# A two-layer hybrid network on one core: the down phase gives VectorE the accumulation alone, and products use six PSUM banks

## The chip, the cores and the metric

The kernel runs on one core of a Trainium2 chip. Five engines work in parallel, each through its own queue in order: TensorE (PE; its weight loads are shown as PEld), VectorE (DVE), ScalarE (ACT), GpSimd (POOL), and SyncE (SP), which here issues nearly all transfers. The metric is the device time of one execution in microseconds (us), the median over runs. "Granted clock" is the share of its full clock that TensorE was given in a stretch.

## The reference

A sequence of 16 learned tokens and 1024 inputs of width 1024 goes through two layers. Each adds a mixer (stick-breaking attention beside an S5 state space model in layer 0, a gated delta rule in layer 1) and then an MLP, all with RMS norms around them. The change concerns the MLP:

```python
def sq_relu_mlp(h, w1, w2):
    return jnp.square(jax.nn.relu(h @ w1)) @ w2

for i in range(DEPTH):
    ...
    hn = rms_norm(hs, pre_mlp_norm[i])
    hs = hs + rms_norm(sq_relu_mlp(hn, mlp_w1[i], mlp_w2[i]), post_mlp_norm[i])
```

`w1` is 1024 x 4096 and `w2` 4096 x 1024, in fp32.

## The kernel before

Activations lie with features on the 128 partitions and tokens along the row: 1040 tokens in layer 0, the last 1024 in layer 1. A matrix product keeps fp32 accuracy by splitting each operand into a high part (the value cast to fp32r) and a low part (the value minus its high part) and adding three matmuls: high x high (L176), high weights x low activations (L177), low weights x high activations (L178). Making one operand takes a cast and a subtraction.

The MLP of a layer (`mlp`, L401) has three phases:

- *Up*: six of the 32 blocks of 128 hidden features go through `up` (L416). A product sums over eight input blocks in one PSUM bank, and VectorE takes relu and scale out of the bank (L422, into a tile `t1`, shown as `t`). Meanwhile `halves_T` makes sums and differences of the inputs (`th`, `tl`) for the next phase.
- *Pairs*: the other 26 blocks are made two at a time by `pair` with seven half-size products instead of eight (L476 to L478). ScalarE casts the weight operands (L437), GpSimd subtracts (L438), VectorE combines the products (L485, L489). These products go round the banks of all three kinds. The squared result goes to `hd` in DRAM.
- *Down*: `down` (L531) is called 14 times with two hidden blocks each and once more with the last four (`last`). Each call loads its hidden blocks (`hidden`, L523: DMA of `hr`, ScalarE's cast to `hh`, VectorE's subtraction to `hl`) and its weights (`weight`, L152: DMA of `wraw`, VectorE's cast to `whi`, GpSimd's subtraction to `wlo`), and then runs over eight blocks of output features. A product is six matmuls (two hidden blocks, three each) in one bank: three products of 352, 344 and 344 tokens per output block in layer 0, two of 512 in layer 1. Call 0 copies each product to `acc` on ScalarE (L550); the later ones add it to `acc` on VectorE (L552).

PSUM has eight banks: three named `mm`, three `tr`, two `ax`. `gemm` (L182), which both up and down use, takes `mm` alone, so a product can start when the product three before it has been taken out. There are two tiles `wraw` and four each of `whi` and `wlo`, so a call's weights are made while the call before it runs; 33 slots hold `hr`, `hh`, `hl` and `acc` with others, so hidden blocks run several calls ahead.

A scheduling layer sets the order on each engine: it spreads the instructions by its own estimate of when each will be ready, and adds the waits. Line numbers below are those of this kernel; a line that many callers share (L165, L166, L176 to L178, L228, L229) stands for all of them, so tile names tell them apart.

Of the kernel before, what the change touches and what calls it, by code (L numbers as in the profile page):

```python
# [19 lines left out]
NT = 1040  # L20
# [26 lines left out]
def f(ap):  # L47
    return ap.bitcast(F32)


class Net:
# [97 lines left out]
    def raw(self):  # L149
        return self.sb.tile([128, NT], F32, tag="wraw", name="wraw", bufs=2)  # L150

    def weight(self, src, n=1024, spare=False, fast=False):  # L152

        nc = self.nc
        raw = self.raw()
        nc.sync.dma_start(raw[:, :n], src)
        if spare:
            hi, lo = self.slot("whi", F32R), self.slot("wlo", F32R)
        else:
            hi = self.sb.tile([128, 1024], F32R, tag="whi", name="whi", bufs=4)  # L160
            lo = self.sb.tile([128, 1024], F32R, tag="wlo", name="wlo", bufs=4)
        if fast and HA:
            nc.scalar.copy(hi[:, :n], raw[:, :n])
        else:
            nc.vector.tensor_copy(hi[:, :n], raw[:, :n])  # L165
        (nc.vector if fast else nc.gpsimd).tensor_sub(lo[:, :n], raw[:, :n], f(hi[:, :n]))  # L166
        return hi, lo
# [11 lines left out]
            self.clock += n / 800  # L179
            self.beat()  # L180

    def gemm(self, mts, kts, wap, rhs, chunks, order, evac, hook=None):  # L182
        mts = list(mts)
        cs = range(len(chunks))
        todo = [(m, c) for m in mts for c in cs] if order == "m" else [(m, c) for c in cs for m in mts]
        for i, (m, c) in enumerate(todo):
            if order == "c" and i == len(mts) * (len(chunks) - 1) and hook is None:
                self.finish()
            o, n = chunks[c]
            pt = self.mm()  # L190
            self.unit(pt[:, :n], kts, lambda k: wap(m, k), rhs, o, n)
            evac(m, c, pt[:, :n])
            if hook is not None:
                hook(m, c)
# [206 lines left out]
    def mlp(self, layer, st, hs_d, chunks, gpre, ahead=None):  # L401

        nc = self.nc
        w1, w2 = self.io["w1"], self.io["w2"]
        hd = self.dr.tile([128, 32, NT], F32, tag="hd%d" % layer, name="hd", bufs=1)
        hid = {}
        t0, h = (0, 520) if layer == 0 else (16, 512)
        half = ((0, 260), (260, 260)) if layer == 0 else ((0, 512),)
        wide = chunks if layer == 0 else CH4

        def put(m, o, n, x):

            nc.scalar.activation(x[:, :n], x[:, :n], AF.Square)
            nc.sync.dma_start(hd[:, m, o:o + n], x[:, :n])

        def up(ms, order):  # L416
            W = self.w_up if ms[0] == 0 else {m: self.weight(w1[layer, m]) for m in ms}

            def ev(m, c, pt):
                o, n = chunks[c]  # L420
                t1 = self.tmp("t1")
                nc.vector.scalar_tensor_tensor(t1[:, :n], pt, 0.0, st["rb"][:, o:o + n], op0=ALU.max, op1=ALU.mult)  # L422
                put(m, o, n, t1)

            self.gemm(ms, range(8), lambda m, k: tuple(w[:, k * 128:(k + 1) * 128] for w in W[m]), lambda k: (st["hi"][k], st["lo"][k]), chunks, order, ev)

        room = []
        bank = cycle((self.mm, self.tr, self.mm, self.tr, self.mm, self.tr, self.ax))
# [32 lines left out]
        def pair(ma, mb, T):  # L461
# [26 lines left out]
            def block(m, o, n, x):  # L488
                nc.vector.scalar_tensor_tensor(x[:, :n], x[:, :n], 0.0, st["rb"][:, o:o + n], op0=ALU.max, op1=ALU.mult)  # L489
                put(m, o, n, x)  # L490
# [32 lines left out]
        def hidden(k):  # L523

            raw = self.slot("hr")
            hi, lo = self.slot("hh", F32R), self.slot("hl", F32R)
            nc.sync.dma_start(raw[:, t0:NT], hd[:, k, t0:NT])
            self.split(hi[:, t0:NT], lo[:, t0:NT], raw[:, t0:NT])
            hid[k] = (hi, lo)

        def down(ks, last=False):  # L531
            first = ks[0] == 0
            for k in ks:
                hidden(k)
            W = {k: self.weight(w2[layer, k]) for k in ks}
            out, hook, ch = None, None, wide
            if last:
                ch = chunks
                if ahead is None:
                    ch = CH3  # L540
                if ahead is not None:
                    ahead()
                ssq = self.slot("ssq_o")
                reuse = [t for k in ks for t in hid[k]]
                *out, hook = self.residual(acc, ssq, reuse, G_POSTMLP + 8 * layer, hs_d, gpre, ch)

            def ev(m, c, pt):
                o, n = ch[c]
                if first:
                    nc.scalar.copy(acc[m][:, o:o + n], pt)  # L550
                else:
                    nc.vector.tensor_add(acc[m][:, o:o + n], pt, acc[m][:, o:o + n])  # L552
                if last:
                    self.sq_acc(ssq, m, m == 0, acc[m][:, o:o + n], o, n)

            self.gemm(range(8), ks, lambda m, k: tuple(w[:, m * 128:(m + 1) * 128] for w in W[k]), lambda k: hid[k], ch, "c" if last else "m", ev, hook)
            for k in ks:
                del hid[k]
            return out

        up([0, 1, 2, 3], "c")
        T = self.halves_T(st, hs_d, t0, h, G_PREMLP + 8 * layer)
        for m in range(4, UPC):
            up([m], "m")
        for m in range(UPC, 32, 2):
            pair(m, m + 1, T)
        acc = [self.slot("acc") for _ in range(8)]
        for g in range(14):
            down([2 * g, 2 * g + 1])
        return down([28, 29, 30, 31], True)  # L570


# [317 lines left out]
    def glu(self):  # L890

        nc = self.nc
        W = [self.weight(self.io["wglu"][i]) for i in range(2)]
        hact = self.hact
# [14 lines left out]

        wap = lambda m, k: tuple(w[:, 512 * (k % 2) + 128 * m:512 * (k % 2) + 128 * m + 128] for w in W[k // 2])  # L910
        for m in range(4):
# [27 lines left out]
    def attention(self, qd, kd, vd, vd0):  # L939
# [123 lines left out]
        units = [(p, pr, h) for p in range(4) for pr in range(4) for h in range(2)]  # L1063
        qk, V, W, osb = {}, {}, {}, []
        for i in range(len(units) + AHEAD):
# [762 lines left out]
HA = 1  # L1828
# [314 lines left out]
```

## Time and profile before

| what | value |
| --- | --- |
| median of 3 runs | 3060.87 us (3060.43 to 3077.38) |
| the profiled execution | 3069.21 us, span 3067.2 us |
| mean granted clock | 0.931 |
| PE busy | 2816.3 us, 92% of the span |
| DVE busy | 1894.7 us, 62% |
| ACT busy | 1020.7 us, 33% |
| POOL busy | 1165.8 us, 38% |
| down phase, layer 0, calls 0 to 13 | 1081 to 1470 us |
| down phase, layer 1, calls 0 to 13 | 2656 to 2999 us |
| up phase, first to last L422 | 740 to 820 us and 2327 to 2402 us |

The page cuts the span into 40 slices of 76.7 us; slices 15 to 19 and 35 to 39 hold the down phases:

```profile
PE   7899999998999989889897978999999999989997
DVE  8634777668555557666656896545537444466655
ACT  4112566655433321000336422444435333311001
POOL 5561234235677621111433123111145777412223
PEclk9889667989999989999998988999999999999999
```

Each digit is the busy share of a slice in tenths; PEclk is the granted clock in tenths. In a row of the timeline stand start, duration, engine, line, operation, tiles and shapes, and in brackets how long the engine stood idle before it and what ended that. A row of a tile or line view has the shortest, median and longest duration in ns. A row of the windows view has, after the stretch and its length, the busy time of PE, PEld, DVE, ACT and POOL, each with its count, then the granted clock, the DMA share and GB/s.

### The profile page before, as it was taken

What the parts mean: (1) busy time and instruction counts of PE and PEld (TensorE: products, weight loads), DVE (VectorE), ACT (ScalarE), POOL (GpSimd) and SP (SyncE); (2) the same over time, 40 slices, a digit from 0 to 9 for tenths busy, and PEclk for the clock granted to TensorE, in tenths of its full rate; (3) what the DMA queues carried; (4) which work ended last, traced back from release to release, by engine and by line L of the source; (5) the groups of instructions that cost most, each with busy time, mean ns of one, the idle gap of its engine ahead of it and who ended that gap; (6) DMA issues with size and microseconds to landing.
All of it is one profiled execution on the core that took longest, in us unless ns stands there. A gap on an engine that the chain in (4) does not pass through costs nothing. (4 is left out here: it accounts for less than half of the span.)

```text
span 3067.2 us, 43940 instructions
## 1 busy us (share of the span) xinstructions
PE 2816.3 (92%) x16488; PEld 2534.5 (83%) x16488; DVE 1894.7 (62%) x3195; ACT 1020.7 (33%) x2084; POOL 1165.8 (38%) x878
## 2 busy tenths in 40 slices
PE   7899999998999989889897978999999999989997
PEld 7688667788899989889887977899988788767777
DVE  8634777668555557666656896545537444466655
ACT  4112566655433321000336422444435333311001
POOL 5561234235677621111433123111145777412223
PEclk9889667989999989999998988999999999999999
DMA  3435221144333333221327567444425233332222
GB/s 129 156 126 150 70 77 56 47 155 137 113 108 100 122 111 111 84 77 42 107 76 217 195 205 231 128 134 135 138 91 166 93 106 110 121 133 96 89 82 84
DMA packets 209763, 360.97 MB, mean 118 GB/s; under 512 B 45488, under 2 KB 131200, under 8 KB 209552
## 3 DMA queue, kind: packets, MB, share of 16 engines
q1 hardware_dynamic: 205664, 353.49, 35.5%
q10 hardware_dynamic: 3888, 4.69, 0.4%
q8 instruction: 130, 2.13, 0.3%
q14 instruction: 81, 0.66, 0.1%
HBM read 247.07 MB, written 111.03 MB: 117 GB/s over the span
## 5 line engine op out<-in xcount | busy, mean ns | idle before, releaser
L166 POOL TENSOR_TENSOR wlo<-wraw,whi 128x1024 fp32r<-128x1024 f32 x129 | 327.9, 2548 | 1102.3 <-DVE whi L165 532.7
L177 PE MATMUL mm<-hl,whi 128*128 128x344 f32 (+4 forms) x1696 | 594.3, 351 | 3.3 <-DVE hl L229 3.2
L176 PE MATMUL mm<-hh,whi 128*128 128x512 f32 (+4 forms) x1312 | 469.6, 359 | 61.7 <-DVE acc L552 45.4
L176 PE MATMUL mm<-ahi,whi 128*128 128x344 f32 (+2 forms) x1344 | 470.0, 350 | 57.4 <-DVE cx L1331 30.1
L178 PE MATMUL mm<-hh,wlo 128*128 128x512 f32 (+4 forms) x1312 | 465.2, 355 | 5.4 <-POOL wlo L166 5.4
L552 DVE TENSOR_TENSOR acc<-mm,acc 128x352 f32<-128x352 f32 (+4 forms) x568 | 321.9, 578 | 229.2 <-PE mm L178 229.0
L178 PE MATMUL mm<-ahi,wlo 128*128 128x344 f32 (+2 forms) x1344 | 449.7, 335 | 2.2 <-DVE wlo L166 2.2
L177 PEld LDWEIGHTS mm<-hl,whi 128*128 128x128 f32 x1696 | 331.7, 196 | 25.1 <-DVE hl L229 4.8
L176 PEld LDWEIGHTS mm<-hh,whi 128*128 128x128 f32 x1312 | 255.0, 195 | 97.1 <-DVE acc L552 58.9
L176 PEld LDWEIGHTS mm<-ahi,whi 128*128 128x128 f32 x1344 | 265.8, 198 | 67.7 <-DVE cx L1331 31.5
L178 PEld LDWEIGHTS mm<-hh,wlo 128*128 128x128 f32 x1312 | 255.9, 195 | 27.0 <-POOL wlo L166 6.6
L178 PEld LDWEIGHTS mm<-ahi,wlo 128*128 128x128 f32 x1344 | 265.0, 197 | 5.2 <-DVE wlo L166 3.4
L228 ACT CAST hh<-hr 128x1040 fp32r<-128x1040 f32 (+1 forms) x64 | 67.6, 1056 | 451.5 <-DMA hr<-hd 264.8
L165 DVE CAST whi<-wraw 128x1024 fp32r<-128x1024 f32 x129 | 117.9, 925 | 105.1 <-PE mm L177 70.3
L438 POOL TENSOR_TENSOR wlo<-sS,whi 128x512 fp32r<-128x512 f32 x104 | 143.1, 1379 | 30.9 <-ACT whi L437 30.8
L177 PE MATMUL mm<-ml,whi 128*128 128x344 f32 (+2 forms) x432 | 140.9, 326 | 0.7 <-DVE ml L229 0.7
L229 DVE TENSOR_TENSOR hl<-hr,hh 128x1040 fp32r<-128x1040 f32 (+1 forms) x64 | 113.9, 1780 | 40.8 <-ACT hh L228 40.8
L177 PE MATMUL mm<-hh,whi 128*128 128x344 f32 (+2 forms) x384 | 130.3, 339 | 0.0
L366 POOL TENSOR_TENSOR ssq_o<-ssq_o,sq 128x344 f32<-128x344 f32 (+4 forms) x84 | 93.9, 1118 | 80.1 <-ACT sq L365 79.6
L244 POOL TENSOR_TENSOR ssq<-ssq,sq 128x344 f32<-128x344 f32 (+2 forms) x84 | 91.2, 1086 | 82.7 <-ACT sq L243 74.6
L995 DVE TENSOR_TENSOR_SCAN keep<-keep,cst 128x400 f32<-128x400 f32 (+5 forms) x72 | 94.7, 1328 | 44.9 <-ACT keep L993 44.5
L438 POOL TENSOR_TENSOR wlo<-wraw,whi 128x512 fp32r<-128x512 f32 x78 | 109.5, 1403 | 26.0 <-ACT whi L437 26.0
(509 smaller groups left out, 6873.9 us busy)
## 6 DMA issues: line engine op xcount, KB each, us to landing
wraw<-w SPq DMA_DIRECT2D x128, 512.0 KB, 3.4
hr<-hd SPq DMA_DIRECT2D x32, 520.0 KB, 4.6
wraw<-wino SPq DMA_DIRECT2D x32, 512.0 KB, 5.3
hr<-hd SPq DMA_DIRECT2D x32, 512.0 KB, 4.3
dm<-dmd SPq DMA_DIRECT2D x16, 520.0 KB, 5.0
hsd<-hs SPq DMA_DIRECT2D x48, 172.0 KB, 1.9
hd<-u SPq DMA_DIRECT2D x52, 130.0 KB, 2.0
hd<-u SPq DMA_DIRECT2D x26, 256.0 KB, 2.0
```

The lines of the kernel that those rows point to most:

```text
L165: nc.vector.tensor_copy(hi[:, :n], raw[:, :n])
L166: (nc.vector if fast else nc.gpsimd).tensor_sub(lo[:, :n], raw[:, :n], f(hi[:, :n]))
L176: nc.tensor.matmul(pt, wh, h[:, o:o + n], start=i == 0, stop=False)
L177: nc.tensor.matmul(pt, wh, l[:, o:o + n], start=False, stop=False)
L178: nc.tensor.matmul(pt, wl, h[:, o:o + n], start=False, stop=i == len(kts) - 1)
L228: nc.scalar.copy(hi, src)
L229: (lo_eng or nc.vector).tensor_sub(lo, src, f(hi))
L244: nc.gpsimd.tensor_add(st["ssq"][:, o:o + n], st["ssq"][:, o:o + n], sq[:, :n])
L366: nc.gpsimd.tensor_add(ssq[:, o:o + n], ssq[:, o:o + n], sq[:, :n])
L438: nc.gpsimd.tensor_sub(lo, src, f(hi))
L552: nc.vector.tensor_add(acc[m][:, o:o + n], pt, acc[m][:, o:o + n])
L995: v.tensor_tensor_scan(kp[:n, 0:L][:, ::-1], kp[:n, 0:L][:, ::-1], self.one_row[:n, :L], 1.0, op0=ALU.mult, op1=ALU.mult)
```

## The change

Three things change, in the down phase but for the third. The weights' casts go from VectorE (L165) to ScalarE (L163). The low parts of the hidden blocks (L229) go from VectorE to GpSimd, and call 0's copies out of PSUM (L550) from ScalarE to VectorE. The products of `up`, and of all calls of `down` but the last, take `mm` and `tr` banks in turn, six in all.

```diff
-    def weight(self, src, n=1024, spare=False, fast=False):
+    def weight(self, src, n=1024, spare=False, fast=False, act=False):
...
-        if fast and HA:
+        if fast and HA or act:
             nc.scalar.copy(hi[:, :n], raw[:, :n])
         else:
             nc.vector.tensor_copy(hi[:, :n], raw[:, :n])
...
-    def gemm(self, mts, kts, wap, rhs, chunks, order, evac, hook=None):
+    def gemm(self, mts, kts, wap, rhs, chunks, order, evac, hook=None, banks=None):
...
-            pt = self.mm()
+            pt = next(banks)() if banks else self.mm()
...
+        six = cycle((self.mm, self.tr))
+
         def put(m, o, n, x):
...
-            self.gemm(ms, range(8), ..., chunks, order, ev)
+            self.gemm(ms, range(8), ..., chunks, order, ev, banks=six)
...
-            self.split(hi[:, t0:NT], lo[:, t0:NT], raw[:, t0:NT])
+            self.split(hi[:, t0:NT], lo[:, t0:NT], raw[:, t0:NT], lo_eng=nc.gpsimd)
...
-            W = {k: self.weight(w2[layer, k]) for k in ks}
+            W = {k: self.weight(w2[layer, k], act=True) for k in ks}
...
-                    nc.scalar.copy(acc[m][:, o:o + n], pt)
+                    nc.vector.tensor_copy(acc[m][:, o:o + n], pt)
...
-            self.gemm(range(8), ks, ..., ch, "c" if last else "m", ev, hook)
+            self.gemm(range(8), ks, ..., ch, "c" if last else "m", ev, hook, None if last else six)
```

In the changed kernel the lines after L411 are two higher. Three places show how the scheduling layer set the moved instructions. The first is VectorE in layer 0 where call 3 begins, before the change (`acc<-mm` is an add; the numbers tell tiles of one name apart):

```order
L552 TENSOR_TENSOR acc_11048<-mm_11689,acc_11048 128x344
L165 CAST whi_11927<-wraw_11925 128x1024
L552 TENSOR_TENSOR acc_11041<-mm_11721,acc_11041 128x352
L165 CAST whi_11933<-wraw_11931 128x1024
L552 TENSOR_TENSOR acc_11041<-mm_11729,acc_11041 128x344
L552 TENSOR_TENSOR acc_11041<-mm_11737,acc_11041 128x344
L229 TENSOR_TENSOR hl_12353<-hr_12351,hh_12352 128x1040
```

The same engine where call 2 begins, after it:

```order
L554 TENSOR_TENSOR acc_11041<-mm_11505,acc_11041 128x352
L554 TENSOR_TENSOR acc_11041<-tr_11513,acc_11041 128x344
L554 TENSOR_TENSOR acc_11041<-mm_11521,acc_11041 128x344
L554 TENSOR_TENSOR acc_11042<-tr_11529,acc_11042 128x352
L554 TENSOR_TENSOR acc_11042<-mm_11537,acc_11042 128x344
```

The two casts and the low part are gone from between the adds, and the adds read the two kinds of banks in turn.

The second is GpSimd at the start of layer 0's down phase; `wlo_11064` and the one after it belong to call 0, `wlo_11280` to call 1, `wlo_11496` to call 2. Before:

```order
L166 TENSOR_TENSOR wlo_11064<-wraw_11061,whi_11063 128x1024
L166 TENSOR_TENSOR wlo_11070<-wraw_11067,whi_11069 128x1024
L166 TENSOR_TENSOR wlo_11280<-wraw_11277,whi_11279 128x1024
L166 TENSOR_TENSOR wlo_11286<-wraw_11283,whi_11285 128x1024
L166 TENSOR_TENSOR wlo_11496<-wraw_11493,whi_11495 128x1024
L166 TENSOR_TENSOR wlo_11502<-wraw_11499,whi_11501 128x1024
```

After, with `hl_11051` and `hl_11057` for call 0, `hl_11267` and `hl_11273` for call 1:

```order
L229 TENSOR_TENSOR hl_11051<-hr_11049,hh_11050 128x1040
L166 TENSOR_TENSOR wlo_11064<-wraw_11061,whi_11063 128x1024
L229 TENSOR_TENSOR hl_11057<-hr_11055,hh_11056 128x1040
L166 TENSOR_TENSOR wlo_11070<-wraw_11067,whi_11069 128x1024
L166 TENSOR_TENSOR wlo_11280<-wraw_11277,whi_11279 128x1024
L166 TENSOR_TENSOR wlo_11286<-wraw_11283,whi_11285 128x1024
L166 TENSOR_TENSOR wlo_11496<-wraw_11493,whi_11495 128x1024
L166 TENSOR_TENSOR wlo_11502<-wraw_11499,whi_11501 128x1024
L229 TENSOR_TENSOR hl_11267<-hr_11265,hh_11266 128x1040
L229 TENSOR_TENSOR hl_11273<-hr_11271,hh_11272 128x1040
```

Call 1's low parts stand behind the low weights of call 2.

The third is ScalarE at the same place, before:

```order
L550 COPY acc_11048<-mm_11241 128x352
L550 COPY acc_11048<-mm_11249 128x344
L550 COPY acc_11048<-mm_11257 128x344
L228 CAST hh_11266<-hr_11265 128x1040
L228 CAST hh_11272<-hr_11271 128x1040
```

After:

```order
L163 CAST whi_11285<-wraw_11283 128x1024
L415 ACTIVATE u2_10869<-u2_10869 128x260
L163 CAST whi_11495<-wraw_11493 128x1024
L163 CAST whi_11501<-wraw_11499 128x1024
L228 CAST hh_11266<-hr_11265 128x1040
L228 CAST hh_11272<-hr_11271 128x1040
```

Call 0's copies are gone from here, and call 2's weight casts, which need call 0's weights to be done with, stand ahead of call 1's hidden blocks.

More of the change, by code (lines that the diff above doesn't have):

```diff
@@ L423, in ev @@
                 put(m, o, n, t1)
-            self.gemm(ms, range(8), lambda m, k: tuple(w[:, k * 128:(k + 1) * 128] for w in W[m]), lambda k: (st["hi"][k], st["lo"][k]), chunks, order, ev)
+            self.gemm(ms, range(8), lambda m, k: tuple(w[:, k * 128:(k + 1) * 128] for w in W[m]), lambda k: (st["hi"][k], st["lo"][k]), chunks, order, ev, banks=six)
         room = []
@@ L554, in ev @@
                     self.sq_acc(ssq, m, m == 0, acc[m][:, o:o + n], o, n)
-            self.gemm(range(8), ks, lambda m, k: tuple(w[:, m * 128:(m + 1) * 128] for w in W[k]), lambda k: hid[k], ch, "c" if last else "m", ev, hook)
+            self.gemm(range(8), ks, lambda m, k: tuple(w[:, m * 128:(m + 1) * 128] for w in W[k]), lambda k: hid[k], ch, "c" if last else "m", ev, hook, None if last else six)
             for k in ks:
```

## Prediction

> **What bounds the kernel.** I read the page first (TensorE is busy 92% of the span, so only its waits are worth anything), then TensorE's waits by stretch, the timeline around one wait, and last the distance between two marks per pass. "Pass" is one call of down() before the last: 14 a layer, 24 products each in layer 0 and 16 in layer 1. TensorE's waits, one stretch per row: passes of layer 0, of layer 1, start of layer 0's first pass, and the up phase of the two layers.
>
> ```profile
> PE mm L176 <- DVE acc L552: 30.5, 20, 2.4
> PE mm L176 <- DVE acc L552: 13.4, 16, 1.9
> PE mm L176 <- ACT acc L550: 3.7, 2, 2.3
> PE mm L176 <- DVE t L422: 7.3, 2, 5.4
> PE mm L176 <- DVE t L422: 5.4, 1, 5.4
> ```
>
> Columns: us in total, times, longest. TensorE waits for an accumulation because a product needs a bank that is not emptied. Why it isn't shows in the timeline of one pass start (start, duration):
>
> ```profile
> 1225.96 2.40 POOL L166 TENSOR_TENSOR wlo<-wraw,whi 128x1024 fp32r<-128x1024 f32 x1 [22.79 <-DVE whi L165]
> 1226.17 2.75 DVE L165 CAST whi<-wraw 128x1024 fp32r<-128x1024 f32 x1
> 1229.05 2.37 POOL L166 TENSOR_TENSOR wlo<-wraw,whi 128x1024 fp32r<-128x1024 f32 x1 [0.68 <-PE mm L178]
> 1229.27 3.24 DVE L229 TENSOR_TENSOR hl<-hr,hh 128x1040 fp32r<-128x1040 f32 x1
> 1229.40 0.43 PE L176 MATMUL mm<-hh,whi 128*128 128x352 f32 x1 [0.91 <-DVE acc L552]
> 1232.43 1.35 DVE L552 TENSOR_TENSOR acc<-mm,acc 128x344 f32<-128x344 f32 x3
> 1232.99 0.49 PE L176 MATMUL mm<-hh,whi 128*128 128x344 f32 x1 [2.36 <-DVE acc L552]
> 1234.00:1236.00 2.00, 2.00 (x9) 2.00 (x8) 0.52 (x1) 0.00 (x0) 0.00 (x0) 0.50 0.75 305
> 1238.00:1240.00 2.00, 2.00 (x14) 2.00 (x13) 1.16 (x3) 0.00 (x0) 0.00 (x0) 1.00 0.00 0
> L165 DVE CAST whi<-wraw x129: 657/685/2746, 17.8 to 2999.3; 128x1024 fp32r<-128x1024 f32 x129
> ```
>
> VectorE's cast and low-part subtraction, while GpSimd works beside them, take 2.75 and 3.24 us (the cast's median is 0.685), the adds queue behind them, three banks hold about 3 us of products, and TensorE stands for 0.91 and then 2.36 us. The two windows (granted clock is third from the end) show a second price: 0.50 at 1234 to 1236, 1.00 again from 1238. So I count whole pass lengths, not waits. The marks are GpSimd's first weight subtraction of a pass:
>
> ```profile
> 1143.79 2.39 POOL L166 TENSOR_TENSOR wlo<-wraw,whi 128x1024 fp32r<-128x1024 f32 x1 [26.75 <-DVE whi L165]
> 1469.69 2.37 POOL L166 TENSOR_TENSOR wlo<-wraw,whi 128x1024 fp32r<-128x1024 f32 x1 [18.66 <-DVE whi L165]
> 2713.45 2.41 POOL L166 TENSOR_TENSOR wlo<-wraw,whi 128x1024 fp32r<-128x1024 f32 x1 [28.44 <-DVE whi L165]
> 2932.85 5.10 POOL L166 TENSOR_TENSOR wlo<-wraw,whi 128x1024 fp32r<-128x1024 f32 x2 [18.14 <-PE mm L178]
> 2955.04 5.10 POOL L166 TENSOR_TENSOR wlo<-wraw,whi 128x1024 fp32r<-128x1024 f32 x2 [17.09 <-PE mm L178]
> 1403.72 0.32 PE L176 MATMUL mm<-hh,whi 128*128 128x352 f32 x1
> 1409.44 0.32 PE L176 MATMUL mm<-hh,whi 128*128 128x352 f32 x1
> ```
>
> Layer 0, passes 2 to 13: 12 passes in 1469.69 - 1143.79 = 325.9 us, 27.16 each. Undisturbed, six products take 1409.44 - 1403.72 = 5.72 us, so 24 take 22.88. Layer 1, passes 2 to 10: 9 in 219.4 us, 24.38 each; the pass after them, in which no low part of activations is left to make and TensorE never waits, takes 2955.04 - 2932.85 = 22.19.
>
> **The change, part by part.** *Passes 2 and later.* Two casts and two subtractions per pass leave VectorE; of its queue only adds remain (24 in layer 0; three took 1.35 us above, so about 12 us of a pass). What blocked it is gone, so each pass falls to its undisturbed length: 12 x (27.16 - 22.88) = 51.4 us in layer 0 and 9 x (24.38 - 22.19) = 19.7 us in layer 1. This needs cover on the other two engines:
>
> ```profile
> 1143.00:1449.00 306.00, 274.60 (x1606) 268.57 (x1605) 214.61 (x316) 24.44 (x23) 55.23 (x24) 0.94 0.23 79
> L163 ACT CAST whi<-wraw x13: 1029/1041/1055, 7.8 to 2323.4; 128x1024 fp32r<-128x1024 f32 x13
> L166 POOL TENSOR_TENSOR wlo<-wraw,whi x129: 2341/2399/3389, 18.6 to 3002.1; 128x1024 fp32r<-128x1024 f32 x129
> 1400.19 1.36 DVE L552 TENSOR_TENSOR acc<-mm,acc 128x352 f32<-128x352 f32 x3
> 1400.40 2.40 POOL L166 TENSOR_TENSOR wlo<-wraw,whi 128x1024 fp32r<-128x1024 f32 x1 [0.68 <-PE mm L178]
> DMA to landing us min/median/max: 3.4/4.5/8.0
> 1114.16 0.38 SPq L527 DMA_DIRECT2D hr<-hd  x1
> 1118.30 1.06 ACT L228 CAST hh<-hr 128x1040 fp32r<-128x1040 f32 x1 [6.13 <-DMA hr<-hd]
> ```
>
> The window row (VectorE, ScalarE, GpSimd are the fourth to sixth figures) has ScalarE at 24.44 and GpSimd at 55.23 of 306 us. ScalarE gets two casts of 1.04 us per pass beside two of 1.06. GpSimd gets two subtractions of 1040 columns; the nearest row is L166 on 1024, 2.40 us (longest 3.39), so it does four in about 9.6 us of 22.9, at worst 13.6. The adds do not pay for it: three took 1.36 us with GpSimd busy beside two of them. Queued behind a late cast on ScalarE are the next passes' casts; behind a late subtraction on GpSimd, the next weights' low parts. The longest dependent chain that I find in the queues, from one pass's weights to the next, is four subtractions, two issues on SP (0.8), one landing of hr (the DMA row, 4.5) and four casts (4.2): 9.6 + 0.8 + 4.5 + 4.2 = 19.1 us, 3 us inside a pass. Its longest rows give 13.6 + 0.8 + 8.0 + 4.2 = 26.6 us; that end feeds the range. I take 19.1, since L166's median is over 129.
>
> *Passes 0 and 1.* The first row is pass 0 of layer 0 (144 matmuls), the rest the start of pass 1, the last the same place in layer 1:
>
> ```profile
> 1081.20:1110.20 29.00, 25.31 (x144) 24.57 (x143) 7.95 (x11) 11.51 (x27) 4.75 (x2) 0.88 0.28 94
> 1111.03 6.01 POOL L166 TENSOR_TENSOR wlo<-wraw,whi 128x1024 fp32r<-128x1024 f32 x2 [22.09 <-DVE whi L165]
> 1119.39 1.24 DVE L229 TENSOR_TENSOR hl<-hr,hh 128x1040 fp32r<-128x1040 f32 x1 [4.58 <-ACT hh L228]
> 2678.92 6.10 POOL L166 TENSOR_TENSOR wlo<-wraw,whi 128x1024 fp32r<-128x1024 f32 x2 [18.65 <-PE mm L178]
> ```
>
> Pass 0 takes 29.0 us at a clock of 0.88 against 22.9: the 3.7 us of waits for L550 and the slow clock after them. Its 24 copies now stand on VectorE, behind the pair phase's last work, with six banks to run ahead. I take 4 of the 6 us (bounds 0 and 6). In pass 1 TensorE waits for its own activations: SP (the row at 1114.16) starts the second hr only once the raw weights ahead of it have room, 4 us after pass 0 ended at 1110.2; the low part is ready 10.4 us after. Changed: cast 1.05, subtraction 2.4, issue 0.4, landing 4.5, cast 1.05, subtraction 2.4: about 12 us. That is 1.5 later, but by then six products instead of three have done their first half (about 1.9 us more). Nothing, between -4 and +3 for each layer; for layer 1 I take 2 us, since the pair of subtractions there took 6.1 us and would take 5.
>
> *Up phase.* Banks alone:
>
> ```profile
> 801.83 4.66 DVE L229 TENSOR_TENSOR tl<-sS,th 128x520 fp32r<-128x520 f32 x4
> 806.98 0.66 PE L176 MATMUL mm<-ahi,whi 128*128 128x352 f32 x1 [5.39 <-DVE t L422]
> 2388.16 0.65 PE L176 MATMUL mm<-ahi,whi 128*128 128x344 f32 x1 [5.43 <-DVE t L422]
> 780.00:1081.00 301.00, 293.69 (x2378) 293.12 (x2376) 168.77 (x311) 115.39 (x245) 206.70 (x151) 0.99 0.36 109
> ```
>
> VectorE makes low parts for the pair phase while TensorE wants a bank; three more hold over 11 us of work there. Waits of 7.3 + 5.4 = 12.7 us go, and 2 us of slow clock (0.66 and 0.65 us for the first product): 14.7. The pair phase behind it has TensorE busy 293.69 of 301, all of its wait being these 7.3, so no later wait takes them back; GpSimd, at 206.7 of 301, has 94 us to spare. Bounds 10 and 17.
>
> *The last pass* keeps three banks and its waits; a cast of 1.04 for one of 0.685 to 2.75: nothing, 1 us either way. The transfers are the same; on SP a few swap places.
>
> Sum: 51.4 + 19.7 + 4 + 2 + 14.7 = 91.8 us. Against the profiled execution's 3069.2: 2977.4. It ran 8.3 us above the median of 3060.9, from which the same sum gives 2969.
>
> **The clock, row and rule.** Above, gaps of 0.91 and 2.36 us were followed by a clock of 0.50, gone by 1238. [...]
>
> **Rivals.** (1) *Only the waits go*: the clock stays low in stretches, since products cycling through banks leave TensorE short gaps. Then 30.5 + 13.4 + 12.7 + 3.7 = 60 us: 3001. [...] Against it: from 1238 the old kernel cycles three banks at 1.00.
>
> (2) *A new wait*: the chain above closes later than the pass. At 26.6 us, 12 passes of layer 0 lose 3.7 and 12 of layer 1 (three of them clean before) 4.4: 97 us. If every second pass meets it, 48 come back: 3017.
>
> (3) *Slower*: GpSimd becomes the bound because VectorE's adds hold it up, at the weights of each pass. With four subtractions of T the chain is 4T + 9.5; the gain of 92 over 24 passes is used up at 22.5 + 3.8 = 26.3 us, T = 4.2. At 5 us it is 29.5, 6.6 and 7.3 over: 167 us more, 3136. For it speaks only the longest 3.39; against it the rows at 2932.85 and 2955.04, where two subtractions beside nothing but adds and two casts took 5.10, 2.55 each.
>
> **Chances.** Forecast 0.70, own range 2950 to 2988; rival 1 0.12; rival 2 0.14; rival 3 0.04. The forecast alone gives 2969. The range for 8 in 10 takes in rival 1 and half a step towards rival 2: 2945 to 3010. Faster by over 1% (under 3030; about what a measurement of this kernel tells from no change) holds the forecast, rival 1 and most of rival 2: 0.90; within 1%, the heavier cases of rival 2: 0.06; slower: 0.04.
>
> **What would show it.** Right: no TensorE wait on L552's successor between passes 2 and 13; marks 22.9 and 22.2 us apart; clock 1.00 there; no wait on t in the up phase; VectorE near 12 us of adds per pass, GpSimd near 10. Wrong: waits on hl or wlo named GpSimd at pass starts (rivals 2 and 3), or marks above 23.5 us with clock below 0.95 and few waits (rival 1). Pass 1 of both layers should still wait about 8 us.

## The result: 3.3% faster, and the passes at TensorE's own length

The changed kernel takes 2964.98 us (median of 4 runs, 2961.22 to 2969.17) against 3061.9 for the kernel before in the same comparison (4 runs, 3060.43 to 3077.38): a ratio of 0.967, 95% interval 0.964 to 0.971. In a second comparison (the ninth kernel below) it was 0.968 (0.966 to 0.971). The forecast was 2969, with 2945 to 3010 as range.

The profiled execution of the changed kernel took 2961.22 us, span 2959.2. Its rows of the page's slices (40 of 74 us; the down phases lie in slices 15 to 19 and 35 to 39):

```profile
PE   7799998999999999999897978999998999999997
DVE  8643778677665555555846995444537444544445
POOL 5561325225577755342522132111135777655423
PEclk9899568899999999999998988999999999999999
```

TensorE now shows 9 in every slice of the passes; before, it had 8 in slices 15, 17, 18 and 36. The windows view of passes 2 and later of layer 0 (columns as before: PE, PEld, DVE, ACT, POOL, then the clock):

```profile
1130.00:1390.00 260.00, 260.00 (x1639) 260.00 (x1639) 141.74 (x273) 44.67 (x44) 107.65 (x45) 1.00 0.27 89
```

TensorE is busy for all of the 260 us at a clock of 1.00. VectorE has 141.74 us of them, which is its adds, ScalarE and GpSimd have 45 and 108. In layer 1 the view gives 201.00 of the 201 us from 2626 to 2827, again at 1.00. The marks (GpSimd's first low weight of passes 2 and 14 in layer 0, of passes 2 and 11 in layer 1):

```profile
1121.24 4.77 POOL L166 TENSOR_TENSOR wlo<-wraw,whi 128x1024 fp32r<-128x1024 f32 x2 [10.60 <-ACT whi L163]
1395.58 4.69 POOL L166 TENSOR_TENSOR wlo<-wraw,whi 128x1024 fp32r<-128x1024 f32 x2 [18.11 <-ACT whi L163]
2626.73 2.42 POOL L166 TENSOR_TENSOR wlo<-wraw,whi 128x1024 fp32r<-128x1024 f32 x1 [8.24 <-ACT whi L163]
2827.44 2.41 POOL L166 TENSOR_TENSOR wlo<-wraw,whi 128x1024 fp32r<-128x1024 f32 x1 [8.86 <-ACT whi L163]
```

That is 274.34 / 12 = 22.86 us per pass in layer 0 and 200.71 / 9 = 22.30 in layer 1. TensorE's waits from pass 0 to the start of pass 2, layer 0 and then layer 1 (us in total, times, longest):

```profile
PE mm L177 <- POOL hl L229: 3.5, 1, 3.5
PE mm L176 <- ACT hh L228: 2.5, 1, 2.5
PE mm L177 <- POOL hl L229: 3.7, 1, 3.7
PE mm L176 <- ACT hh L228: 2.2, 1, 2.2
```

Only pass 1 still waits, and for its own hidden blocks. In the up phases no wait for `t` is left.

Between the two profiled executions the spans differ by 108.0 us. The marks, and the first relu and the first down matmul of each layer, cut this into parts (us that the changed kernel is shorter):

| part | layer 0 | layer 1 |
| --- | --- | --- |
| ahead of the up phase | 6.7 | 1.8 (from layer 0's last call on) |
| up and pair phases | 9.2 | 6.9 |
| pass 0 | 6.3 | 0.2 |
| pass 1 | 0.4 | 3.8 |
| passes 2 to 13, or 2 to 10 | 51.6 | 18.7 |
| passes 11 to 13 | | 0 |
| last call | (in the 1.8) | 2.6 |

The first row, 8.5 us, is not counted as gain of the change below: nothing was changed ahead of layer 0's up phase, and the 1.8 us hold, of what was changed, only the casts and low parts of layer 0's last call.

### The profile page after: what moved, and what is told of

It is laid out like the page before. It is cut to its first block, busy times and chain, and to the rows that moved or that the text cites. A ratio compares the mean times of both kernels' runs of the same rounds, so it can differ in the third digit from the quotient of the medians.

```text
span 2959.2 us, 44165 instructions
## 1 busy us (share of the span) xinstructions
PE 2771.1 (94%) x16488; PEld 2506.0 (85%) x16488; DVE 1764.7 (60%) x3107; ACT 1064.4 (36%) x2108; POOL 1311.6 (44%) x942
## 5 line engine op out<-in xcount | busy, mean ns | idle before, releaser
L177 PE MATMUL mm<-hl,whi 128*128 128x352 f32 (+4 forms) x1136 | 388.8, 342 | 7.2 <-POOL hl L229 7.2
L554 DVE TENSOR_TENSOR acc<-mm,acc 128x344 f32<-128x344 f32 (+4 forms) x308 | 177.3, 576 | 198.2 <-PE mm L178 198.2
L176 PE MATMUL mm<-hh,whi 128*128 128x352 f32 (+4 forms) x752 | 260.0, 346 | 5.3 <-ACT hh L228 4.6
L178 PE MATMUL mm<-hh,wlo 128*128 128x352 f32 (+4 forms) x752 | 259.9, 346 | 5.0 <-POOL wlo L166 5.0
L177 PEld LDWEIGHTS mm<-hl,whi 128*128 128x128 f32 x1136 | 218.1, 192 | 19.6 <-POOL hl L229 8.4
L554 DVE TENSOR_TENSOR acc<-tr,acc 128x344 f32<-128x344 f32 (+2 forms) x260 | 152.9, 588 | 137.2 <-PE tr L178 137.2
L163 ACT CAST whi<-wraw 128x1024 fp32r<-128x1024 f32 x77 | 77.5, 1044 | 361.1 <-PE tr L177 357.9
L177 PE MATMUL tr<-hl,whi 128*128 128x512 f32 (+2 forms) x560 | 197.2, 352 | 0.0
L178 PE MATMUL tr<-hh,wlo 128*128 128x512 f32 (+2 forms) x560 | 197.1, 352 | 0.0
L176 PE MATMUL tr<-hh,whi 128*128 128x512 f32 (+2 forms) x560 | 196.9, 352 | 0.0
L229 POOL TENSOR_TENSOR hl<-hr,hh 128x1040 fp32r<-128x1040 f32 (+1 forms) x64 | 155.2, 2434 | 84.6 <-ACT hh L228 69.3
```

Of the source, the lines that this page charges most:

```text
L176: nc.tensor.matmul(pt, wh, h[:, o:o + n], start=i == 0, stop=False)
L177: nc.tensor.matmul(pt, wh, l[:, o:o + n], start=False, stop=False)
L178: nc.tensor.matmul(pt, wl, h[:, o:o + n], start=False, stop=i == len(kts) - 1)
L229: (lo_eng or nc.vector).tensor_sub(lo, src, f(hi))
```

## The experiments

Each ratio is to the kernel before on the same chip. Lines are those of the changed kernel.

**1. Banks alone.** Six banks as in the changed kernel; casts, low parts and copies put back.

```diff
-            self.split(hi[:, t0:NT], lo[:, t0:NT], raw[:, t0:NT], lo_eng=nc.gpsimd)
+            self.split(hi[:, t0:NT], lo[:, t0:NT], raw[:, t0:NT])
-            W = {k: self.weight(w2[layer, k], act=True) for k in ks}
+            W = {k: self.weight(w2[layer, k]) for k in ks}
-                    nc.vector.tensor_copy(acc[m][:, o:o + n], pt)
+                    nc.scalar.copy(acc[m][:, o:o + n], pt)
```

> Edit: the kernel before with six banks in the up phase and in the passes, every cast, subtraction and copy where it was. Theory A (VectorE's blocks are shorter than what six banks hold: five products ahead are 4.8 us, the longest block seen is 3.24 us and two follow each other within 6.3 us): the up waits go (about 15 us) and most waits on an accumulation too, a pass of layer 0 at 23 to 24 us, 2970 to 2985 us. Theory B (the moves are needed: two blocks and the adds queued behind them outlast six banks): up gains 15 us, passes of layer 0 stay at 26 us or more with the wait at the second block, 3020 to 3035 us.

Measured: 2981.26 us, ratio 0.972 (0.968 to 0.975). Theory A: passes of layer 0 take 23.48 us, of layer 1 22.27. VectorE's timeline in a pass of this kernel, and the product that TensorE starts late behind it:

```profile
1241.01 2.75 DVE L165 CAST whi<-wraw 128x1024 fp32r<-128x1024 f32 x1
1244.12 3.27 DVE L229 TENSOR_TENSOR hl<-hr,hh 128x1040 fp32r<-128x1040 f32 x1
1247.86 0.43 PE L176 MATMUL tr<-hh,whi 128*128 128x344 f32 x1 [0.73 <-DVE acc L554]
```

TensorE's waits in this kernel from 1120 to 1400 us are these alone:

```profile
PE tr L176 <- DVE acc L554: 6.0, 9, 0.7
```

VectorE's two blocks are there as before, 6.4 us from 1241.01 to 1247.39 with one add between them. Six products take 5.72 us, and 0.7 us is what is left to wait, once in a pass and in nine passes. The clock of passes 2 to 13 is 1.00. So bank depth by itself takes 44 of the 52 us of layer 0's passes (12 x (27.16 - 23.48)) and all of layer 1's.

**2. Moves alone.** The changed kernel with three banks everywhere (`banks=six` and `None if last else six` removed).

> Edit: the changed kernel with three banks everywhere, up and down. Theory A (the moves empty VectorE's queue, an add of 0.45 us per product of 0.95 us needs no more than three banks): passes of layer 0 at 22.9 us, the up phase waits 12.7 us for t as before, 2978 to 2984 us. Theory B (three banks are too few even so): waits on the add stay, passes above 24 us, 3000 us or more.

Measured: 2990.59 us, ratio 0.975 (0.972 to 0.979). Theory A holds for the passes (22.84 and 22.23 us, no wait for an add from 1120 to 1400 us) and for the up phase, but the whole is 7 us over its range. Some of this may be the chip, on which the kernel before took 3067.08 us, 5 more than in the first comparison. In the trace the place is pass 1. It takes 34.7 and 35.9 us, against 32.8 and 34.5 before the change and 32.4 and 30.8 with six banks; TensorE's waits in pass 0 and pass 1 of layer 0 here:

```profile
PE mm L177 <- POOL hl L229: 4.6, 2, 3.9
PE mm L176 <- ACT hh L228: 2.5, 1, 2.5
PE mm L176 <- DVE acc L552: 1.3, 1, 1.3
```

So the moves make pass 1 longer by 1.9 and 1.4 us, and six banks win back 2.3 and 5.1. Only 1.1 and 1.3 us of that are shorter waits (7.1 us in pass 1 of layer 0 and 7.2 of layer 1 with three banks, 6.0 and 5.9 with six); the rest is the clock after them. The windows view of layer 1's pass 1, with three banks and then with six:

```profile
2612.51:2648.41 35.90, 28.96 (x98) 21.70 (x99) 11.05 (x17) 8.17 (x9) 18.73 (x8) 0.76 0.31 117
2595.96:2626.73 30.77, 25.18 (x98) 19.70 (x99) 10.57 (x17) 8.19 (x9) 18.82 (x8) 0.89 0.36 137
```

The same 98 matmuls keep TensorE busy for 28.96 us at a clock of 0.76 and for 25.18 at 0.89.

**3. Three banks in the up phase alone** (`banks=six` removed there).

> Edit: the changed kernel with three banks in the up phase alone. Theory: the up term stands by itself; two waits on t of about 5 us each and a shorter one come back, in the up phase of both layers, about 15 us: 2978 to 2984 us, and the down phase is as in the changed kernel. Rival: the low parts of the pair phase are late anyway, so the wait only moves behind the up phase: 2965 to 2970 us.

Measured: 2981.15 us, ratio 0.971 (0.968 to 0.974). As the theory: the up and pair phases are 6.2 and 6.8 us longer than with six banks, the passes are those of the changed kernel (22.86, 22.30). Of the waits for `t`, one came back in each layer; the shorter third one did not:

```profile
PE mm L176 <- DVE t L424: 4.5, 1, 4.5
PE mm L176 <- DVE t L424: 4.9, 1, 4.9
```

**4 and 10. Pass 1's hidden blocks asked for early.** In the changed kernel pass 1's blocks stand behind pass 2's weights on two queues. SP's timeline around pass 1, and then ScalarE's:

```profile
1072.65 0.37 SPq L529 DMA_DIRECT2D hr<-hd  x1
1091.26 0.33 SPq L156 DMA_DIRECT2D wraw<-w  x1
1091.69 0.37 SPq L529 DMA_DIRECT2D hr<-hd  x1
```

```profile
1087.75 1.99 ACT L163 CAST whi<-wraw 128x1024 fp32r<-128x1024 f32 x2 [17.77 <-PE tr L177]
1089.65 1.05 ACT L228 CAST hh<-hr 128x1040 fp32r<-128x1040 f32 x1
```

The first `hr` was asked for at 1072.65, but its cast waits on ScalarE behind two weight casts that need pass 0's weights to be done with; the second `hr` waits on SP for room in `wraw`. The edit:

```diff
-            for k in ks:
+            for k in [k for k in (range(4) if first else ks) if k not in hid]:
                 hidden(k)
```

> Edit: the changed kernel with the hidden blocks of pass 1 asked for together with those of pass 0, so that they stand ahead of pass 2's weights on the queues of SP, ScalarE and GpSimd. Theory (pass 1 waits because its second hidden block is queued on SP behind a raw weight tile that is not free until pass 0 ends): pass 1 falls from 32.4 to about 23 us in layer 0 and from 30.8 to about 22.3 us in layer 1, 15 to 18 us in all, 2947 to 2951 us. Rival (the slots of the pair phase, or the block's transfer, are late anyway; or the earlier blocks take GpSimd's or SP's time from the pair phase): 2960 to 2970 us.

Measured: 2952.57 us, ratio 0.962 (0.959 to 0.966), an interval that touches that of the changed kernel. The time is 1.6 us over the theory's range and 7 under the rival's. So both kernels were measured again in one comparison.

> Edit: none, the changed kernel again, to stand beside the next one on the same chip. Expected of either theory: 2960 to 2972 us.

> Edit: the fourth kernel again (hidden blocks of pass 1 asked for early), with more rounds. Theory: its gain over the changed kernel is pass 1's wait, 9.6 us in layer 0 and 8.6 in layer 1, less 0.7 in layer 0's pass 0: 17 us, 2944 to 2954 us, interval clear of the changed kernel's. Rival: the difference of the first comparison (12 to 16 us, intervals that touch) was the chip's spread: within 5 us of the changed kernel.

Measured: 2968.48 us, ratio 0.968 (0.966 to 0.971), for the changed kernel, and 2948.65, ratio 0.962 (0.959 to 0.964), for the early blocks: 20 us less, intervals apart, as the theory had it. Passes 0 and 1 of layer 0 in the first profile of it, by the windows view:

```profile
1072.67:1096.84 24.17, 23.79 (x151) 23.50 (x150) 17.39 (x29) 6.07 (x11) 9.93 (x5) 1.00 0.38 133
1096.84:1119.56 22.72, 22.72 (x146) 22.72 (x145) 12.46 (x24) 7.21 (x8) 16.83 (x7) 1.00 0.45 164
```

Pass 1 is now as long as the others (22.72; 22.19 in layer 1), and pass 0 gives 0.7 us back in layer 0. With the eighth kernel, from which it can't be told apart, this is the fastest of the study.

**5. Casts alone** (three banks; only the weights' casts go to ScalarE: `act=True`) and **6. low parts alone** (three banks; only `lo_eng=nc.gpsimd`), both on the kernel before.

> Edit: the kernel before with the weights' casts on ScalarE alone; three banks, low parts and copies as before. Theory (the two casts cause the shorter wait of about 0.9 us at a pass start, the low parts the longer one of 2.4 us, and VectorE's backlog adds them up): most of a pass's loss stays with the low parts, passes of layer 0 at 24.5 to 26 us; waits and up phase unchanged elsewhere; 3015 to 3040 us. Rival (neither block matters alone, since one of them by itself fits three banks): passes near 23 us, 2985 to 3000 us.

> Edit: the kernel before with the hidden blocks' low parts on GpSimd alone; three banks, casts and copies as before. Theory: the casts' shorter waits stay, at most 0.9 us each, and the clock is not lowered by them; passes of layer 0 at 23 to 24.5 us, pass 1 some 2 us longer than before; 2990 to 3010 us. Rival (the casts, which run beside GpSimd's subtractions at 2.75 us each, are the main block): passes above 25 us, 3020 us or more.

Measured: 3029.58 us, ratio 0.990 (0.988 to 0.991), and 3014.89, ratio 0.985 (0.984 to 0.987). Casts alone came out within its theory's figures; low parts alone did so in the passes, with a total at 5 us over. Layer 0's passes take 25.36 and 24.04 us (12 passes each), layer 1's 23.92 and 22.26. The block on VectorE is of another kind in each. With the casts moved, VectorE's timeline in one pass and the product behind it:

```profile
1253.63 1.24 DVE L229 TENSOR_TENSOR hl<-hr,hh 128x1040 fp32r<-128x1040 f32 x1 [3.04 <-ACT hh L228]
1255.36 0.50 PE L176 MATMUL mm<-hh,whi 128*128 128x352 f32 x1 [2.46 <-DVE acc L554]
```

With the low parts moved:

```profile
1256.72 2.75 DVE L165 CAST whi<-wraw 128x1024 fp32r<-128x1024 f32 x1
1259.95 0.43 PE L176 MATMUL mm<-hh,whi 128*128 128x352 f32 x1 [0.93 <-DVE acc L554]
```

In the first, the low part itself takes only 1.24 us, with GpSimd not at work (it had ended at 1247.74); but VectorE, in order, stands 3.04 us for its input `hh`, and the adds queue behind that. In the second, a cast takes 2.75 us beside GpSimd, and TensorE waits 0.93. Neither move alone empties VectorE's queue; both together do (the second kernel).

**7 and 11. More work for GpSimd.** The changed kernel with the low part of a hidden block made three times over, and two times over. The first:

```diff
             self.split(hi[:, t0:NT], lo[:, t0:NT], raw[:, t0:NT], lo_eng=nc.gpsimd)
+            for _ in range(2):
+                nc.gpsimd.tensor_sub(lo[:, t0:NT], raw[:, t0:NT], f(hi[:, t0:NT]))
```

> Edit: the changed kernel with each low part of a hidden block made three times over on GpSimd, so that a pass asks 8 subtractions of GpSimd (19.2 us) instead of 4. Theory A (the dependent chain of the prediction closes once in every pass, so what GpSimd takes longer is paid as soon as the chain of 19.1 us passes the pass): chain 28.7 us, 5.8 us more in each of 12 passes of layer 0 and 6.5 in each of 12 of layer 1, 3090 to 3120 us. Theory B (hidden blocks run several passes ahead, so only GpSimd's total counts, and 19.2 us fit into 22.2 to 22.9): passes 2 and later unchanged, but pass 1, which has no block in hand, 5 to 10 us longer in each layer: 2975 to 2990 us.

Measured: 3057.45 us, ratio 0.997 (0.996 to 0.999): 92 us over the changed kernel, between the two theories. The windows view of passes 1, 2, 3 and 5 of layer 0 shows what both had missed (GpSimd is the last of the five engines):

```profile
1108.22:1159.65 51.43, 38.68 (x217) 38.11 (x218) 17.93 (x35) 11.14 (x11) 50.49 (x21) 0.83 0.25 94
1159.65:1201.13 41.48, 34.56 (x219) 34.27 (x217) 19.21 (x37) 7.21 (x7) 40.85 (x19) 0.95 0.25 90
1201.13:1240.13 39.00, 26.44 (x144) 25.69 (x144) 12.46 (x24) 5.08 (x5) 38.30 (x18) 0.81 0.20 68
1259.74:1279.58 19.84, 19.84 (x127) 19.84 (x126) 10.90 (x21) 4.02 (x4) 19.45 (x9) 1.00 0.31 107
```

GpSimd is full in passes 1 to 3, with 18 to 21 instructions each, and from pass 5 on a pass asks for 8 subtractions, which fit into 19.8 us, so it catches up. The changed kernel has the same shape at a third of the load. Its passes 1, 2, 3 and 4:

```profile
1088.87:1121.24 32.37, 27.01 (x149) 26.57 (x150) 11.91 (x24) 8.26 (x9) 19.08 (x8) 0.84 0.36 132
1121.24:1143.88 22.64, 22.64 (x146) 22.64 (x145) 12.44 (x24) 7.22 (x8) 16.89 (x8) 1.00 0.45 165
1143.88:1166.73 22.85, 22.85 (x146) 22.85 (x145) 12.45 (x25) 7.21 (x8) 16.93 (x8) 1.00 0.43 142
1166.73:1189.62 22.89, 22.89 (x146) 22.89 (x145) 12.46 (x25) 4.13 (x5) 9.60 (x5) 1.00 0.34 115
```

GpSimd's timeline at the last of these marks:

```profile
1166.73 4.78 POOL L166 TENSOR_TENSOR wlo<-wraw,whi 128x1024 fp32r<-128x1024 f32 x2 [0.97 <-ACT whi L163]
```

When the slots come free after the pair phase, hidden blocks are loaded ahead in a burst, 6, 5 and 5 low parts in three passes, and GpSimd had been idle for only 0.97 us before pass 4's weights. The second kernel of the pair was laid out from this:

> Edit: the changed kernel with each low part of a hidden block made twice on GpSimd. Theory (GpSimd falls behind only in passes 1 to 3, where its queue holds 6, 5 and 5 low parts besides the two of the weights, and has about one pass of lead to lose): these passes ask 33.6, 28.8 and 28.8 us of GpSimd instead of 19.2, 16.8 and 16.8; of the excess of some 19 us over the lengths they had, the lead of 17 us takes most, so 0 to 4 us per layer, and pass 1 waits 2.4 to 5 us longer for its own low parts: 2970 to 2985 us. Rival (what the thrice-made parts cost, 92 us, grows evenly with the subtractions added): half of it, 3010 us.

Measured: 2974.67 us, ratio 0.970 (0.968 to 0.973): 6 to 10 us over the two medians of the changed kernel, as the theory said, and far from the rival's 3010. By the marks it takes 3.6 and 1.1 us more in pass 0 of the two layers, and 2.4 and 1.9 from pass 1 to the last call, 2.2 of them in layer 0's pass 1. So half of the 9.0 us lies in pass 0, which the theory did not name.

**8. The last call too.** The fourth kernel, with six banks in the last call and the low weights of hidden block 30 on VectorE.

```diff
-            W = {k: self.weight(w2[layer, k], act=True) for k in ks}
+            W = {k: self.weight(w2[layer, k], fast=k == 30, act=True) for k in ks}
-            ..., ch, "c" if last else "m", ev, hook, None if last else six)
+            ..., ch, "c" if last else "m", ev, hook, six)
```

> Edit: as the fourth kernel (hidden blocks of pass 1 asked for early), and in the last call of down six banks too and the low weights of hidden block 30 on VectorE. Theory: the last call's waits for low weights (1.4 and 1.1 us in layer 0, 1.3 and 1.2 in layer 1) and for a bank behind ScalarE's square (3.4 us) go: 6 to 8 us from the fourth kernel's time, 2941 to 2947 us. Rival (the low part on VectorE beside GpSimd takes over 3 us, and the last call's end is set by the norm behind it, not by its products): 2950 to 2956 us.

Measured: 2949.13 us, ratio 0.963 (0.960 to 0.966), beside 0.962 (0.959 to 0.966) for the fourth kernel. A gain of a few us is neither shown nor ruled out; the 6 to 8 that were expected did not come. TensorE's waits in layer 0's last call of this kernel:

```profile
PE ax L203 <- POOL ssq_o L366: 6.3, 3, 5.2
PE ax L221 <- DVE diag L214: 4.8, 2, 2.9
PE mm L178 <- POOL wlo L166: 1.3, 1, 1.3
```

In the fourth kernel these three took 4.6, 0.4 and 2.5 us, and the wait behind ScalarE's square 3.4 more, which is gone here. The first two belong to the norm behind the products and are 6.1 us longer now, so by these views the wait moved there, as the rival said. In each layer one of the two waits for low weights stayed.

## Why the prediction was right, and where its steps were off

**Passes 2 and later** (51.4 and 19.7 us) came as 51.6 and 18.7. The mechanism named, adds queued behind the casts and low parts on VectorE, is shown by the fifth and sixth kernels, each of which leaves one block and its wait, and by the second, which removes both without a bank. What the step did not see is that the change holds two cures for it: it put the passes' gain down to the moves and costed the banks there at nothing, yet the first kernel shows that banks alone give 44 of those 52 us in layer 0 and all of layer 1's.

**Up phase** (14.7): 9.2 + 6.9 = 16.1 between the two profiles, 13.0 by the third kernel, where nothing else differs from the changed one. The step is right: banks alone. The profiles can be trusted to some 3 us here: layer 0's two phases took 331.6 us in the changed kernel's first profile and 334.5 in its second.

**Pass 0** (4, bounds 0 to 6): 6.3 in layer 0, just past the upper bound, 0.2 in layer 1. Here too either cure alone gives much of the 6.3 us: the second kernel's pass 0, without the banks, takes 25.1 us against 29.8, the first kernel's, without the moves, 26.6.

**Pass 1** (nothing in layer 0, 2 in layer 1): 0.4 and 3.8. The two opposite terms were right in kind: the moves cost 1.9 and 1.4, the banks give 2.3 and 5.1. In layer 1 the second was mis-sized: the step took about 1.9 us for the first halves of products that six banks let TensorE do ahead, and left out the slow clock, which made 3.8 of the 5.1 us (28.96 against 25.18 us of TensorE in the second kernel's experiment). About 8 us of waits were to remain in pass 1; 6.0 and 5.9 did.

**The cover on GpSimd** is the step that failed, without harm to the sum. It said that GpSimd makes four subtractions per pass, 9.6 us of 22.9, and built on them a chain of 19.1 us that had to close in every pass. In passes 1 to 3 it makes 8, 7 and 7, 19.08, 16.89 and 16.93 us, so the cover was thinnest in passes that the step did not look at; and the chain does not close in every pass, since blocks run ahead. That no new wait came in passes 2 and later was therefore right for another reason than the 3 us that the step named. With the low parts doubled that chain would be 23.9 us and cost 1.0 us in each of 12 passes of layer 0 and 1.7 in 12 of layer 1, 32 us; 6 to 10 were measured. The same burst also means that the point given for the third rival, 4.2 us for a subtraction, belongs to the steady pass alone. How slow one would have to be in the burst was tried only through the number of subtractions.

**The rivals.** That only the waits go was wrong: the clock is 1.00 in passes 2 and later of both layers, with six banks in turn. The new wait on GpSimd did not appear in passes 2 and later; with the hidden blocks' subtractions made three times over, the time was still 0.997 of that before.

**The clock.** In the prediction's rows a clock of 0.50 follows two gaps, of 0.91 and 2.36 us. In the fifth kernel it follows a lone gap of 2.46 us. The windows after the gap at 1255.36 above, and after one of 2.29 us in the same kernel that ended at 1229.66 (the clock is third from the end):

```profile
1257.00:1259.00 2.00, 2.00 (x9) 2.00 (x8) 0.52 (x1) 0.00 (x0) 0.00 (x0) 0.50 0.37 150
1259.00:1261.00 2.00, 2.00 (x15) 2.00 (x14) 1.03 (x2) 0.00 (x0) 0.00 (x0) 1.00 0.00 0
1231.00:1233.00 2.00, 2.00 (x15) 2.00 (x14) 1.14 (x3) 0.00 (x0) 0.00 (x0) 1.00 0.49 196
```

The gaps of 0.9 us in the sixth kernel left it at 1.00 in layer 0's passes from 2 to 13. So the long gap can carry the second price by itself; what the 0.91 us ahead of it added is not shown. In one place of the kernel before, layer 0's last call, it looks as if gaps added up: two of 1.29 and 1.35 us stand there, each shorter than lone gaps of up to 1.74 us that left the clock at 1.00, and the window behind the second has 0.59:

```profile
1472.11 0.43 PE L178 MATMUL mm<-hh,wlo 128*128 128x352 f32 x1 [1.29 <-POOL wlo L166]
1475.14 0.43 PE L178 MATMUL mm<-hh,wlo 128*128 128x352 f32 x1 [1.35 <-POOL wlo L166]
1475.20:1477.20 2.00, 2.00 (x8) 2.00 (x9) 0.53 (x1) 0.00 (x0) 0.00 (x0) 0.59 0.53 139
```

But two of 1.01 and 1.44 us in a pass of layer 0 of that kernel, ending at 1176.36 and 1179.98, left it at 1.00 from 1180 to 1183, so that gaps add up is not shown. Counting pass lengths instead of waits was right in either case.

**The sum.** Between the profiles the changed parts (the table above without its first row) add up to 99.7 us against the sum's 91.8. The excess lies in pass 0 (2.5), pass 1 (2.2), the up phase (1.4) and the last call (2.6), less 0.8 in the passes. The medians differ by 96.9, and by 99.6 in the second comparison.

## What to carry to other kernels

When an engine empties PSUM in order, find the longest stretch in which it does something else, beside the time that the banks hold: here 6.4 us against 2.9 with three banks and 5.7 with six, which leaves 3.5 and 0.7 us (measured: 0.91 and 2.36 together, and 0.73). Either cure, more banks or less work on that engine, would have brought most of the gain, so each should be tried alone before both are kept. When work is moved to an idle engine, look at its load in the burst after buffers come free and not at a steady pass (19 us in pass 1 against 9.6 later). And look at what the change leaves: the remaining wait of pass 1 was the order of two queues, and asking for two blocks earlier was worth another 20 us.

## What the runs showed of the hardware

- In these runs the length of a gap does not decide the clock alone. In passes 2 and later of the kernel before and of the first, fifth and sixth kernels, lone gaps up to 1.74 us (ending at 2754.24 in the kernel before) left it at 1.00; all eight of 2.34 to 2.37 us in layer 0's passes of the kernel before, each 3.6 us behind one of 0.9, were followed by 0.50, for 2.6 to 5.5 us and in four of the eight for 3.2 (PE's timeline: matmuls of 344 and 352 columns start 0.28 to 0.30 us apart there, and 0.15 to 0.17 at 1.00). For lone gaps from 1.9 to 2.5 us both occur: 0.50 followed 1.95 us in the kernel before (at 2720.68 us) and 2.46 in the fifth (1255.36); 1.00 followed 2.24 in the first kernel (1074.50), and 2.29 and once 2.46 in the fifth (1229.66 and 2724.26). The changed kernel itself shows it best. At the start of its first up phase it has a wait of 1.98 us (ending at 730.43) in one profile and of 1.97 (740.46) in the other; behind the first the clock is 1.00, behind the second 0.68, and from its first to its last relu the phase took 70.4 and 73.3 us:

```profile
731.00:734.00 3.00, 3.00 (x20) 2.90 (x19) 2.91 (x6) 2.56 (x6) 1.73 (x3) 1.00 0.50 137
741.00:744.00 3.00, 3.00 (x14) 2.89 (x14) 2.92 (x6) 2.56 (x6) 1.72 (x3) 0.68 0.40 105
```

What tells these cases apart is not shown.

- In the pass start shown in the prediction, VectorE's cast and its low part took 2.75 and 3.24 us, each with a subtraction of GpSimd beside it. The subtractions ended 2.19 and 2.15 us after these began, and 0.56 and 1.09 us remained. A cast's median is 0.685 us, and the low part at 1253.63 in the fifth kernel, with GpSimd not at work, took 1.24. The adds, which read one operand from PSUM, took 0.52 us each in the changed kernel from 1125 to 1135 us, beside GpSimd's subtractions and between them.
- The changed kernel's first up phase began at 733.74 us in one profile and at 743.76 in another, in a part that no edit touches. That is as large as some of the effects here, which is why parts were compared from mark to mark.
